# A hybrid decoder trunk on one core: the source of 48 adding transfers, and the place of a quarter's first Strassen step

## The chip, the cores and the metric

The kernel runs on one core of a Trainium2 chip. The core has TensorE (matmuls, PE in the profile, its weight loads PEld), VectorE (DVE), ScalarE (ACT), GpSimd (POOL), the sequencer SyncE (SP), which here issues plain loads, and 16 DMA engines, which all queues share. The metric is the device time of one execution in microseconds, the median over several runs.

## What is computed

The reference is a decoder of two layers over 256 tokens of width 2048, all in fp32. The first layer mixes tokens with a convolution module beside differential attention, the second with a gated short convolution. Each layer then attends to 256 memory tokens and applies an MLP whose hidden width is 8192:

```python
def sq_relu_mlp(h, w1, w2):
    return jnp.square(jax.nn.relu(h @ w1)) @ w2

for l in range(DEPTH):                     # DEPTH = 2, D_MODEL = 2048, D_FF = 8192, SEQ = 256
    hn = rms_norm(x, mix_norm_g[l])
    x = x + (even_mixer(hn, ...) if l % 2 == 0 else odd_mixer(hn, ...))
    x = x + cross_attention(rms_norm(x, xattn_norm_g[l]), mem_n, ...)
    x = x + sq_relu_mlp(rms_norm(x, mlp_norm_g[l]), mlp_w1[l], mlp_w2[l])
return rms_norm(x, final_norm_g)
```

## The kernel before

**Split numbers.** The kernel hands TensorE its factors as fp32r, a rounded fp32. To keep fp32's exactness each factor is split into `hi`, its rounded part, and `lo`, the rest, and a product is hi x hi + lo x hi + hi x lo. For a piece of weights (128 x 1024 floats, 512 KB) the helper `weights` (L152 to L170) loads `raw` from DRAM on SP's queue, ACT casts it to `whi` (L164), and DVE subtracts, `wlo = raw - whi` (L169). Of `raw` there are five buffers, of `whi` and `wlo` three each. In the order of the program a load waits until the last reader of its buffer is done.

**The adding transfer.** With `added` set, `wlo` is made without DVE: ACT writes `-raw` into it (L166), and POOL issues a DMA that adds the same piece of weights, from DRAM, onto it (L167). As both are written in fp32r, what stays is the rest. Only the second piece of 48 calls is made so, one in each Strassen step.

**A chunk.** `proj_long` makes 128 output columns from two such pieces: fifteen matmuls with `whi` (tokens' hi and lo side by side, 512 columns), sixteen with `wlo` (256 columns: hi alone), and one last with `whi`.

**The MLP** (`mlp`, L824) goes through the hidden width in four quarters, `qd`. Sixteen chunks c = 0 to 15 make a quarter's hidden activations; after each, DVE adds the two halves (L216) and multiplies (L834), ACT squares (L836). After every fourth, ACT and DVE split the result (`hid`, L840 and L841), and for Strassen's sums DVE combines it in place (L740 to L743) and splits that too (`hs`, L745 and L746). In the first three quarters eight Strassen steps follow. A step takes 256 hidden columns and multiplies half of the output (`w2[:NS]`) by seven products instead of eight: `seven_weights` loads two pieces, `raws`, combines and splits them into `shi`, `slo`, `b22` and two `tw` (L767 to L777), each single or double as the pools give, and 21 matmuls into seven PSUM banks `p` use them. Then a chunk into the bank `mmn`, with the adding transfer, makes the other half. Two layers with three such quarters give 48 steps. `shi` and `slo` share the three buffers of `whi` and `wlo`, `raws` the five of `raw`; `tw` and `b22` have one buffer each.

**What sets the order.** A scheduler puts each engine's instructions in one fixed order when the program is built: by their place in the program and by when buffers come free in its own reckoning. Where `strict` is set, PE keeps the program's order. Every engine then runs its list strictly in that order, each instruction waiting for its semaphores; SP's list holds all plain loads, so a load that waits holds up those behind it.

**Around it.** `spread` (L276) makes two diagonal tiles `diag` on ACT and multiplies each by ones on PE, to lay a row over all partitions.

Of the kernel before, what the change touches and what calls it, by code (L numbers as in the profile page):

```python
# [10 lines left out]
F32 = mybir.dt.float32  # L11
# [3 lines left out]
ALU = mybir.AluOpType  # L15
AX = mybir.AxisListType

P = 128
D = 2048
S = 256  # L20
# [7 lines left out]
NEG = -3.0e38  # L28
# [17 lines left out]
def trunk(ctx: ExitStack, tc: tile.TileContext, d):  # L46
    nc = tc.nc
    V, A, T, G = nc.vector, nc.scalar, nc.tensor, nc.gpsimd

    const = ctx.enter_context(tc.tile_pool(name="const", bufs=1))  # L50
# [4 lines left out]
    tmp = ctx.enter_context(tc.tile_pool(name="tmp", bufs=2))  # L55
    small = ctx.enter_context(tc.tile_pool(name="small", bufs=4))
    pools = {}
# [18 lines left out]
    for n in (2048, 1024, 128):  # L76
        onec[n] = const.tile([P, 1], F32, name=f"onec{n}")
        G.memset(onec[n], 1.0 / n)
    mask = const.tile([P, 2, P], F32, name="mask")
    G.memset(mask, 0.0)  # L80
    zero = small.tile([P, 1], F32, name="zero", bufs=1)
    V.memset(zero, 0.0)
    A.copy(zero, zero)
    G.affine_select(out=mask[:, 1], in_=mask[:, 1], compare_op=ALU.is_ge, fill=-NEG, base=0,
                    pattern=[[-1, P]], channel_multiplier=1)

    def col(name, c=0):
        i = VEC[name] + c
        return gvec[:, i:i + 1] if i < NG else vec[:, i - NG:i - NG + 1]
# [5 lines left out]
    def load_vec():  # L95
        nc.sync.dma_start(out=vec, in_=d["vec"][:, NG:])
        lv = vec[:, VEC["lam"] - NG:VEC["lam"] - NG + 256].rearrange("p (a b) -> p a b", a=4)
        lp = tmp.tile([P, S], F32, tag="t32", name="lp", bufs=6)[:, :128].rearrange("p (a b) -> p a b", a=2)
        V.tensor_tensor(lp, lv[:, 0:4:2], lv[:, 1:4:2], op=ALU.mult)
        ls = small.tile([P, 2], F32, name="ls", bufs=1)  # L100
        V.reduce_sum(out=ls, in_=lp, axis=AX.X)
        le = small.tile([P, 2], F32, name="le", bufs=1)
        A.activation(le, ls, AF.Exp)
        V.tensor_tensor(neglam, le[:, 1:2], le[:, 0:1], op=ALU.subtract)
        V.tensor_scalar(neglam, neglam, -LAM0, None, op0=ALU.add)
        V.tensor_scalar(subg, col("subln_g"), 1.0 - LAM0, None, op0=ALU.mult)
# [12 lines left out]
    def ordered(i, token):  # L119

        tc.stamp_issue_order_token(i.ins, token)
# [30 lines left out]
    def weights(src, added=False):  # L152

        run_later(rate[0], calls[0])
        run_stages(calls[0])
        calls[0] += 1
        raw = wraw.tile([P, 1024], F32, tag="raw", name="raw")
        hi = wspl.tile([P, 1024], F32R, tag="whi", name="whi")
        lo = wspl.tile([P, 1024], F32R, tag="wlo", name="wlo")
        n = 512 if calls[0] == 1 else 1024  # L160
        for i in range(0, 1024, n):
            o = slice(i, i + n)
            nc.sync.dma_start(out=raw[:, o], in_=src[:, o])
            A.copy(hi[:, o], raw[:, o])  # L164
            if added:
                A.activation(lo[:, o], raw[:, o], AF.Copy, scale=-1.0)  # L166
                G.dma_start(out=lo[:, o], in_=src[:, o], accum_op=ALU.add)  # L167
            else:
                ordered(V.tensor_tensor(lo[:, o], raw[:, o], f(hi[:, o]), op=ALU.subtract), "lo")  # L169
        return hi, lo  # L170
# [105 lines left out]
    def spread(rows):  # L276
        ps = ps_nm.tile([P, 512], F32, tag="nm", name="nmb")[:, :S]
        for t in range(2):
            dg = tmp.tile([P, P], F32, tag="diag", name="diag", bufs=1)
            A.activation(dg, ident, AF.Copy, scale=rows[:, t:t + 1])  # L280
            mm(ps[:, t * P:(t + 1) * P], ones, dg, start=True, stop=True)
        return ps
# [18 lines left out]
        return y  # L301

    def to_sbuf(ps, pool=None, name="rb"):
        r = pool.tile([P, S], F32, tag=name, name=name) if pool else tmp.tile([P, S], F32, tag="rb", name=name, bufs=2)
        A.copy(r, ps)
        return r

# [15 lines left out]
            V.tensor_tensor(self.acc, self.acc, sq, op=ALU.add)  # L323

    def tmp32(name="t32"):
        return tmp.tile([P, S], F32, tag="t32", name=name, bufs=6)

    def residual(k, ps, nxt, ss, gname):

# [15 lines left out]
        return softmax_from(src, nm, width, scale)  # L345

    def softmax_from(src, bias, width, scale):
        p = pools["att"].tile([P, S], F32, tag="pexp", name="pexp", bufs=3)
        sm = small.tile([P, 1], F32, tag="psum", name="psum")
        A.activation(p[:, :width], src, AF.Exp, bias=bias, scale=scale, accum_out=sm)  # L350
        inv = small.tile([P, 1], F32, tag="pinv", name="pinv")
        V.reciprocal(inv, sm)
        return p, inv
# [4 lines left out]
    def even_mixer():  # L358
        xa, ss = Act(NC, "xn"), SumSq()
        w = d["even_in"]  # L360

        def load_x(g):
            nc.sync.dma_start(out=x[:, 2 * g:2 * g + 2], in_=d["xT"][:, 2 * g:2 * g + 2])
# [22 lines left out]
        rc, r = rr["col"], rr["bc"]  # L386
        for n, pp in enumerate(pps):
            for t in range(2):
                o = slice(n * 512, (n + 1) * 512)
# [103 lines left out]
        a = half.tile([P, NA, S], F32, tag="half", name="a")  # L493
# [234 lines left out]
    NS = 8  # L728
# [54 lines left out]
                "t1": flat(t1[:, 0, 0], t1[:, 1, 0]), "t4": flat(t1[:, 0, 1], t1[:, 1, 1]),  # L783
                "t3": flat(t2[:, 0, 0], t2[:, 1, 0]), "t2": flat(t2[:, 0, 1], t2[:, 1, 1])}

    def seven_step(pp, src, sa, s, first, last):
        b = seven_weights(src)
        for i, a, w in ((1, sa.single(2 * s, 0), "b11"), (2, sa.single(2 * s + 1, 0), "b21"),
                        (5, sa.comb(1, s), "t1"), (4, sa.single(2 * s + 1, 1), "t4"), (3, sa.comb(4, s), "b22"),
                        (7, sa.comb(3, s), "t3"), (6, sa.comb(2, s), "t2")):  # L790
            mm(pp[i], a[0], b[w][0], start=first, stop=False)
            mm(pp[i], a[1], b[w][0], start=False, stop=False)
            mm(pp[i], a[0], b[w][1], start=False, stop=last)

    def seven_sum(pp, acc):

        (c11, c12), (c21, c22) = [[acc[:, i, j * 512:(j + 1) * 512] for j in range(2)] for i in range(2)]
        u = pools["mlp"].tile([P, 512], F32, tag="u", name="u", bufs=2)
        A.copy(u, pp[1])
        for out, other, op in ((c11, u, ALU.add), (c11, pp[2], ALU.add), (c12, pp[5], ALU.add),  # L800
                               (c22, pp[5], ALU.add), (c21, pp[4], ALU.subtract), (c12, pp[3], ALU.add),
                               (u, pp[6], ALU.add), (c12, u, ALU.add), (u, pp[7], ALU.add), (c21, u, ALU.add),
                               (c22, u, ALU.add)):
            V.tensor_tensor(out, out, other, op=op)
# [19 lines left out]
    def mlp(l, xa, ss, gname):  # L824
        r = rstd(ss.acc, D)
        nxt = nss = None
        w1, w2 = d[f"w1{l}"], d[f"w2{l}"]
        uu = half.tile([P, 2, 2, 4, P], F32, tag="half", name="uu")
        for qd in range(4):
            hid = Act(NC, "hid")  # L830
            sa = SevenAct(hid) if qd < 3 else None
            for c in range(NC):
                u = summed(proj_long(w1[qd * NC + c], xa))
                V.scalar_tensor_tensor(u, u, 0.0, r, op0=ALU.max, op1=ALU.mult)  # L834
                v = uu[:, c // 4 % 2]
                A.activation(v[:, c % 4 // 2, c % 2 * 2:c % 2 * 2 + 2].rearrange("p h f -> p (h f)"), u, AF.Square)  # L836
                if c % 4 == 3:
                    t = hid.t[c // 4]
                    w = v.rearrange("p a (o h) f -> p (a o) (h f)", o=2)
                    A.copy(t[:, :, 0], w)  # L840
                    V.tensor_tensor(t[:, :, 1], w, f(t[:, :, 0]), op=ALU.subtract)  # L841
                    if sa:
                        sa.combine(c // 4, v)
                if c == 1 and qd == 0:
                    acc = turned(True)
                if c == 3 and qd == 3:
                    turned(False)
            cols = slice(qd * D, (qd + 1) * D)
            if qd < 3:
                pp = {i: (ps_mm if i < 5 else ps_at).tile([P, 512], F32, tag="mm" if i < 5 else "at", name=f"p{i}")  # L850
                      for i in range(1, 8)}
                strict[0] = True
                for s in range(8):
                    o = qd * D + s * 2 * P
                    seven_step(pp, w2[:NS, :, o:o + 2 * P], sa, s, s == 0, s == 7)
                    ps = ps_nm.tile([P, 512], F32, tag="nm", name="mmn")
                    residual(NS + s, proj_long(w2[NS + s][:, cols], hid, ps, True), None, None, gname)
                seven_sum(pp, acc)
                strict[0] = False
                continue  # L860
            nxt, nss = Act(NC, "xn") if l == 0 else None, SumSq()
            for c in range(NC):
                residual(c, proj_long(w2[c][:, cols], hid), nxt, nss, gname)
        return nxt, nss
# [14 lines left out]
    r = spread(rstd_rows(ss.acc, D))  # L879
    for g in range(8):  # L880
        o = slice(2 * g, 2 * g + 2)
# [62 lines left out]
```

## Time and profile before

| | |
|---|---|
| median of three runs | 3023.36 us (3022.45 to 3029.5) |
| profiled execution | 3020.86 us, span 3019.1 us |
| PE busy | 2903.0 us (96%) |
| DVE / ACT / POOL busy | 2206.7 / 1605.4 / 45.0 us |
| mean granted TensorE clock | 0.99 |
| read from HBM | 560.3 MB |
| adding transfers | 48, 512 KB each, 8.5 us from issue to landing (median) |
| six stretches of eight Strassen steps | 618.1 us |

The span is the time between the first and last instruction in the trace. In rows of groups, a line, an engine, an operation and its tiles (written <- read) are followed by busy time, mean duration and idle time with what ended it. In rows of the timeline come the start in us, the length (over all of the row's instructions) and in brackets the idle time ahead of it with its releaser; SPq is SP's queue of issues. Rows by windows give, for each stretch, the busy time of each engine, the granted clock (PEclk), the mean busy share of the DMA engines and what they moved in GB/s. Rows of DMA queues give packets, MB and the share of the engines' time: q1 holds SP's plain loads, q0 POOL's transfers.

### The profile page before, as it was taken

To read this page: it belongs to the slowest core of one execution; us is meant where nothing else is said; L and a number is where in the kernel's file an instruction comes from. 1 tells how busy PE (TensorE), PEld (TensorE's weight loads), DVE (VectorE), ACT (ScalarE), POOL (GpSimd) and SP (SyncE) were. 2 spreads that over 40 slices of the span, in tenths; PEclk is the share of its full clock that TensorE was granted. 3 is DMA by queue.
4 is the path that set the end of the run, shared out by engine and by line. 5 is a ranking of instruction groups with operands and counts; after the bars stand their busy time and mean duration, and the time that the engine had idled before them with its cause. 6 is when DMAs were issued, how large, how long until landed. Compare 5 with 4: busy or idle time off the path is not lost.

```text
span 3019.1 us, 42397 instructions
## 1 busy us (share of the span) xinstructions
PE 2903.0 (96%) x16072; PEld 2521.6 (84%) x16072; DVE 2206.7 (73%) x3414; ACT 1605.4 (53%) x2275; POOL 45.0 (1%) x68
## 2 busy tenths in 40 slices
PE   9999999999989989999999999999999899899998
PEld 7888888888877878778888888888888787787887
DVE  7899987777776876766777765477667778777665
ACT  6665455555554545555544444455556546455453
POOL 0000000000000000000000000000000000000000
PEclk9999999999999999999999999999999999999999
DMA  7454565545576685766665656654455766757664
GB/s 242 158 198 154 181 182 189 162 151 186 182 208 187 189 222 174 206 193 188 186 194 196 202 193 193 191 189 160 153 182 181 211 191 198 202 189 212 189 187 138
DMA packets 194172, 565.17 MB, mean 187 GB/s; under 512 B 17456, under 2 KB 66736, under 8 KB 193968
## 3 DMA queue, kind: packets, MB, share of 16 engines
q1 hardware_dynamic: 187056, 537.30, 56.5%
q0 software_dynamic: 6912, 25.17, 4.3%
q8 instruction: 126, 2.06, 0.3%
q14 instruction: 78, 0.64, 0.1%
HBM read 560.30 MB, written 2.10 MB: 186 GB/s over the span
## 4 chain that ended last, share of the span: by engine, by line
PE 80%; DMA 14%; ACT 3%; DVE 2%; issue 1%; SPq 0%; ACTq 0%; DVEq 0%; POOLq 0%
PE mm L143 66%; DMA wlo<-w 13%; PE mmr L143 7%; PE mmn L143 3%; PE p L143 2%; ACT wlo L166 1%; PE pox L143 1%; PE sx L143 1%; ACT whi L164 1%; DVE wlo L169 0%; PE nmb L143 0%; ACT tw L776 0%; DVE slo L768 0%; DVE cv L511 0%; PE nmr L143 0%
## 5 line engine op out<-in xcount | busy, mean ns | idle before, releaser
L169 DVE TENSOR_TENSOR wlo<-raw,whi 128x1024 fp32r<-128x1024 f32 (+1 forms) x865 | 1057.0, 1222 | 457.5 <-PE mm L143 169.6
L164 ACT CAST whi<-raw 128x1024 fp32r<-128x1024 f32 (+1 forms) x913 | 958.4, 1050 | 667.4 <-PE mm L143 271.6
L143 PE MATMUL mm<-xn,whi 128*128 128x512 f32 x3840 | 941.8, 393 | 0.0
L143 PEld LDWEIGHTS mm<-xn,whi 128*128 128x128 f32 x3840 | 704.0, 189 | 133.5
L143 PEld LDWEIGHTS mm<-xn,wlo 128*128 128x128 f32 x3840 | 500.7, 191 | 23.7
L143 PE MATMUL mm<-xn,wlo 128*128 128x256 f32 x3840 | 508.4, 282 | 0.0
L215 ACT COPY sum<-mm 128x256 f32<-128x256 f32 x272 | 101.1, 372 | 569.0 <-PE mm L143 568.8
L143 PE MATMUL mmn<-hid,whi 128*128 128x512 f32 x768 | 192.1, 392 | 0.0
L216 DVE TENSOR_TENSOR sum<-mm,sum 128x256 f32<-128x256 f32 x272 | 115.0, 423 | 98.3 <-ACT sum L215 97.7
L143 PE MATMUL mmn<-hid,wlo 128*128 128x256 f32 x768 | 116.1, 296 | 72.2 <-DMA wlo<-w 72.1
L143 PEld LDWEIGHTS mmn<-hid,wlo 128*128 128x128 f32 x768 | 104.5, 196 | 85.7 <-DMA wlo<-w 81.9
L143 PEld LDWEIGHTS mmn<-hid,whi 128*128 128x128 f32 x768 | 145.3, 189 | 28.2
L777 DVE TENSOR_TENSOR tw<-raws,tw 128x1024 fp32r<-128x1024 f32 x96 | 114.2, 1220 | 41.3 <-ACT tw L776 41.3
L143 PE MATMUL mmr<-whi,mem 128*128 128x512 f32 x512 | 137.4, 390 | 0.0
L143 PE MATMUL p<-tw,hs 128*128 128x512 f32 x432 | 120.4, 402 | 13.1 <-ACT tw L776 6.9
L143 PE MATMUL mm<-mem,whi 128*128 128x512 f32 x512 | 126.3, 393 | 0.0
L143 PE MATMUL mm<-o,whi 128*128 128x512 f32 x512 | 124.7, 392 | 0.0
L143 PE MATMUL mm<-hid,whi 128*128 128x512 f32 x512 | 122.7, 391 | 0.0
L143 PEld LDWEIGHTS p<-tw,hs 128*128 128x128 f32 x432 | 83.9, 195 | 38.0 <-DVE tw L777 11.0
L511 DVE SCALAR_TENSOR_TENSOR cv<-a,vec,cv 128x255 f32<-128x255 f32 (+14 forms) x240 | 111.7, 465 | 3.4
L143 PEld LDWEIGHTS mmr<-whi,mem 128*128 128x128 f32 x512 | 95.8, 188 | 19.7
L143 PEld LDWEIGHTS mm<-hid,whi 128*128 128x128 f32 x512 | 94.1, 188 | 18.6 <-DVE hid L841 0.5
(208 smaller groups left out, 3304.7 us busy)
## 6 DMA issues: line engine op xcount, KB each, us to landing
raw<-w SPq DMA_DIRECT2D x416, 512.0 KB, 4.0
raws<-w SPq DMA_DIRECT2D x96, 512.0 KB, 3.9
raw<-odd_in SPq DMA_DIRECT2D x96, 512.0 KB, 4.3
raw<-even_in SPq DMA_DIRECT2D x64, 512.0 KB, 4.3
raw<-xk SPq DMA_DIRECT2D x64, 512.0 KB, 3.7
raw<-xv SPq DMA_DIRECT2D x64, 512.0 KB, 3.6
raw<-xq SPq DMA_DIRECT2D x64, 512.0 KB, 3.8
raw<-xo SPq DMA_DIRECT2D x64, 512.0 KB, 3.7
```

The lines of the kernel that those rows point to most:

```text
L143: i = T.matmul(*a, **k)
L164: A.copy(hi[:, o], raw[:, o])
L166: A.activation(lo[:, o], raw[:, o], AF.Copy, scale=-1.0)
L169: ordered(V.tensor_tensor(lo[:, o], raw[:, o], f(hi[:, o]), op=ALU.subtract), "lo")
L215: A.copy(t, ps[:, S:])
L216: V.tensor_tensor(t, ps[:, :S], t, op=ALU.add)
L511: ordered(V.scalar_tensor_tensor(cv[:, c, s:], a[:, c, :S - s], col("conv_a_w", i + j), cv[:, c, s:], op0=ALU.mult, op1=ALU.add), "lo")
L777: V.tensor_tensor(t[:, 1], b, f(t[:, 0]), op=ALU.subtract)
```

## The change

1. The adding transfer reads `raw`, the tile on chip, instead of the same piece in DRAM. Its buffer is thereby read until the transfer is through.
2. `seven_weights` is called outside `seven_step`; that of a quarter's first step is called in the loop over chunks, after chunk 12, instead of after chunk 15.
3. Buffers: `t32` 7 instead of 6, `diag` 2 instead of 1, `rb` 3 instead of 2, `pexp` 4 instead of 3, `u` 1 instead of 2. The `mask` of the causal attention is made in the pool of the attention stage instead of among the constants.

```diff
-    mask = const.tile([P, 2, P], F32, name="mask")
-    G.memset(mask, 0.0)
...
-                G.dma_start(out=lo[:, o], in_=src[:, o], accum_op=ALU.add)
+                G.dma_start(out=lo[:, o], in_=raw[:, o], accum_op=ALU.add)
...
-            dg = tmp.tile([P, P], F32, tag="diag", name="diag", bufs=1)
+            dg = tmp.tile([P, P], F32, tag="diag", name="diag")
...
-        r = pool.tile([P, S], F32, tag=name, name=name) if pool else tmp.tile([P, S], F32, tag="rb", name=name, bufs=2)
+        r = pool.tile([P, S], F32, tag=name, name=name) if pool else tmp.tile([P, S], F32, tag="rb", name=name, bufs=3)
...
-        return tmp.tile([P, S], F32, tag="t32", name=name, bufs=6)
+        return tmp.tile([P, S], F32, tag="t32", name=name, bufs=7)
...
-        p = pools["att"].tile([P, S], F32, tag="pexp", name="pexp", bufs=3)
+        p = pools["att"].tile([P, S], F32, tag="pexp", name="pexp", bufs=4)
...
+        mask = pools["att"].tile([P, 2, P], F32, name="mask", bufs=1)
+        G.memset(mask, 0.0)
...
-    def seven_step(pp, src, sa, s, first, last):
-        b = seven_weights(src)
+    def seven_step(pp, b, sa, s, first, last):
...
-        u = pools["mlp"].tile([P, 512], F32, tag="u", name="u", bufs=2)
+        u = pools["mlp"].tile([P, 512], F32, tag="u", name="u", bufs=1)
...
+                if c == 12 and sa:
+                    b = seven_weights(w2[:NS, :, qd * D:qd * D + 2 * P])
...
-                    o = qd * D + s * 2 * P
-                    seven_step(pp, w2[:NS, :, o:o + 2 * P], sa, s, s == 0, s == 7)
+                    if s:
+                        o = qd * D + s * 2 * P
+                        b = seven_weights(w2[:NS, :, o:o + 2 * P])
+                    seven_step(pp, b, sa, s, s == 0, s == 7)
```

PE's list hardly changes. Two places in the lists of the other engines do. The first is SP's list in the steps 1 and 2 of the first quarter, before; `raws` are the two pieces of a step's combined weights, `raw` the two of its chunk, and the names in brackets are semaphores: DMAHW of plain loads, DMASW of POOL's transfers.

```order
L760 DMA raws_8682<-w20 128x4x256 [waits DMAHW2_49,DVE_49]
L760 DMA raws_8683<-w20 128x4x256 [waits DMAHW5_49,DVE_49]
L163 DMA raw_8725<-w20 128x1024 [waits DMAHW4_49,DVE_49,Activation_49]
L163 DMA raw_8731<-w20 128x1024 [waits DMAHW6_49,Activation_49]
L760 DMA raws_8772<-w20 128x4x256 [waits DMAHW3_49,DVE_49]
L760 DMA raws_8773<-w20 128x4x256 [waits DMAHW1_49,DVE_49]
L163 DMA raw_8815<-w20 128x1024 [waits DMAHW7_49,DVE_49]
L163 DMA raw_8821<-w20 128x1024 [waits DMAHW2_49,Activation_49]
```

And the same rows of the changed kernel:

```order
L760 DMA raws_8682<-w20 128x4x256 [waits DMAHW2_49,DVE_49]
L760 DMA raws_8683<-w20 128x4x256 [waits DMAHW3_49,DVE_49]
L159 DMA raw_8725<-w20 128x1024 [waits DMAHW4_49,DVE_49]
L159 DMA raw_8731<-w20 128x1024 [waits DMAHW5_49,DVE_49]
L760 DMA raws_8772<-w20 128x4x256 [waits DMAHW6_49,DMASW0_49,Activation_49]
L760 DMA raws_8773<-w20 128x4x256 [waits DMAHW0_49,DVE_49]
L159 DMA raw_8815<-w20 128x1024 [waits DMAHW7_49,DVE_49]
L159 DMA raw_8821<-w20 128x1024 [waits DMAHW1_49,DVE_49]
```

The first `raws` of step 2 now waits for a DMASW, the landing of step 0's adding transfer; so does the first of each later step, two transfers back, and the three loads behind it come after it in the list. Before, a load of each step waited for ACT's copy instead.

The second place is DVE's list where the first step's weights stand, before: from the end of chunk 14's sum on.

```order
L768 TENSOR_TENSOR slo<-raws,shi 128x1024
L769 TENSOR_TENSOR raws<-raws 128x4x128
L771 TENSOR_TENSOR raws<-raws 128x4x128
L773 TENSOR_TENSOR raws<-raws 128x4x128
L169 TENSOR_TENSOR wlo<-raw,whi 128x1024
L774 TENSOR_TENSOR raws<-raws 128x4x128
L216 TENSOR_TENSOR sum<-mm,sum 128x256
L777 TENSOR_TENSOR tw<-raws,tw 128x1024
L834 SCALAR_TENSOR_TENSOR sum<-sum,rb 128x256
L777 TENSOR_TENSOR tw<-raws,tw 128x1024
```

And in the changed kernel, where `slo`, two `raws` and the split of `hid` stand ahead of this piece, right behind the sum of chunk 11:

```order
L740 TENSOR_TENSOR uu<-uu 128x2x128
L773 TENSOR_TENSOR raws<-raws 128x4x128
L741 TENSOR_TENSOR uu<-uu 128x2x128
L212 TENSOR_TENSOR sum<-mm,sum 128x256
L742 TENSOR_TENSOR uu<-uu 128x2x128
L833 SCALAR_TENSOR_TENSOR sum<-sum,rb 128x256
L743 TENSOR_TENSOR uu<-uu 128x2x128
L774 TENSOR_TENSOR raws<-raws 128x4x128
L777 TENSOR_TENSOR tw<-raws,tw 128x1024
L746 TENSOR_TENSOR hs<-uu,hs 128x8x128
L777 TENSOR_TENSOR tw<-raws,tw 128x1024
L165 TENSOR_TENSOR wlo<-raw,whi 128x1024 x3
```

The sum in it is that of chunk 12. The three `wlo` behind it are the two of chunk 13 and the first of chunk 14; before, a `wlo` stood in the middle of the piece.

More of the change, by code (lines that the diff above doesn't have):

```diff
@@ L83, in trunk @@
     A.copy(zero, zero)
-    G.affine_select(out=mask[:, 1], in_=mask[:, 1], compare_op=ALU.is_ge, fill=-NEG, base=0,
-                    pattern=[[-1, P]], channel_multiplier=1)
     def col(name, c=0):
@@ L97, in load_vec @@
         lv = vec[:, VEC["lam"] - NG:VEC["lam"] - NG + 256].rearrange("p (a b) -> p a b", a=4)
-        lp = tmp.tile([P, S], F32, tag="t32", name="lp", bufs=6)[:, :128].rearrange("p (a b) -> p a b", a=2)
+        lp = tmp.tile([P, S], F32, tag="t32", name="lp", bufs=7)[:, :128].rearrange("p (a b) -> p a b", a=2)
         V.tensor_tensor(lp, lv[:, 0:4:2], lv[:, 1:4:2], op=ALU.mult)
@@ L360, in even_mixer @@
         w = d["even_in"]
+        mask = pools["att"].tile([P, 2, P], F32, name="mask", bufs=1)
+        G.memset(mask, 0.0)
+        G.affine_select(out=mask[:, 1], in_=mask[:, 1], compare_op=ALU.is_ge, fill=-NEG, base=0,
+                        pattern=[[-1, P]], channel_multiplier=1)
         def load_x(g):
```

## The prediction

> **What bounds the kernel now.** I read the page's first part, then the waits of PE, then the step stretches by windows, one step in the timeline, and the DMA queues.
>
> ```profile
> PE 2903.0 (96%) x16072; PEld 2521.6 (84%) x16072; DVE 2206.7 (73%) x3414; ACT 1605.4 (53%) x2275; POOL 45.0 (1%) x68
> PE mmn L143 <- DMA wlo<-w: 72.1, 46, 3.7
> PE nmb L143 <- ACT diag L280: 11.7, 14, 2.9
> PE p L143 <- ACT tw L776: 6.9, 6, 1.1
> PE p L143 <- DVE tw L777: 6.2, 10, 0.7
> ```
>
> PE is busy for 96%, so PE bounds nearly all of it, and a gain can come only out of the 116 us in which it isn't (3019.1 - 2903.0). The waits (us in total, times, longest) say where these are: 72.1 us for the adding transfer, 13.1 us for the first combined weights of a quarter (6.9 + 6.2), 11.7 us for the diagonal tile.
>
> ```profile
> core 0: us, PE busy (x) PEld busy (x) DVE busy (x) ACT busy (x) POOL busy (x), PEclk, DMA share, GB/s
> 835.99:939.74 103.75, 87.65 (x426) 73.03 (x425) 76.78 (x100) 54.53 (x60) 6.97 (x8) 0.98 0.79 213
> 2336.43:2441.01 104.58, 90.46 (x426) 74.77 (x425) 76.55 (x100) 54.48 (x60) 6.82 (x8) 0.95 0.77 207
> ...
> sum 618.14, PE 532.84 PEld 442.16 DVE 459.82 ACT 326.82 POOL 41.02; mean PE 88.81 PEld 73.69 DVE 76.64 ACT 54.47 POOL 6.84
> 939.74:1029.66 89.92, 89.92 (x512) 79.26 (x512) 65.78 (x88) 50.25 (x70) 0.00 (x0) 0.99 0.56 176
> ```
>
> The first rows are two of the six stretches of eight Strassen steps, the sum is that of all six: 618.14 us, 103.0 each. The last row is sixteen chunks between two of them: PE never idles there, and a chunk takes 89.92 / 16 = 5.6 us. So the stretches hold nearly everything that can be won. One step of them:
>
> ```profile
> 861.33 0.38 SPq L760 DMA_DIRECT2D raws<-w  x1
> 862.47 3.53 SPq L163 DMA_DIRECT2D raw<-w  x2
> 863.14 0.40 PE L143 MATMUL mmn<-hid,whi 128*128 128x512 f32 x1
> 863.62 1.05 ACT L164 CAST whi<-raw 128x1024 fp32r<-128x1024 f32 x1 [2.62 <-issue]
> 864.57 1.06 ACT L166 ACTIVATE wlo<-raw 128x1024 fp32r<-128x1024 f32 x1
> 865.92 0.85 POOL L167 DMA_DIRECT2D wlo<-w  x1 [11.40 <-ACT wlo L166]
> 866.09 7.92 SPq L760 DMA_DIRECT2D raws<-w  x2
> 868.15 3.56 PE L143 MATMUL mmn<-hid,whi 128*128 128x512 f32 x15
> 871.55 1.11 PE L143 MATMUL mmn<-hid,wlo 128*128 128x256 f32 x8
> 872.38 2.36 DVE L777 TENSOR_TENSOR tw<-raws,tw 128x1024 fp32r<-128x1024 f32 x2 [1.17 <-ACT tw L776]
> 874.16 1.21 PE L143 MATMUL mmn<-hid,wlo 128*128 128x256 f32 x8 [1.49 <-DMA wlo<-w]
> 875.21 0.40 PE L143 MATMUL mmn<-hid,whi 128*128 128x512 f32 x1
> ```
>
> A step ends with its lone whi matmul: 863.54, then 875.61, so 12.07 us, of which PE waits 1.49 and works 10.6. The wait closes a ring: the last matmul frees a whi buffer, ACT casts and copies (863.62 to 865.63), POOL issues at 865.92, the transfer lands at 874.16, nine matmuls follow. 8.2 us of it is the transfer.
>
> ```profile
> q1 hardware_dynamic: 570, 0.97, 92.2%
> q0 software_dynamic: 144, 0.52, 82.8%
> q1 hardware_dynamic: 105, 0.09, 8.4%
> q0 software_dynamic: 32, 0.13, 58.8%
> 8.00:20.00 12.00, 11.92 (x47) 9.09 (x47) 10.94 (x21) 11.89 (x25) 0.00 (x0) 1.00 1.03 407
> raws<-w SPq DMA_DIRECT2D x96, 512.0 KB, 3.9
> 1241.13 0.86 POOL L167 DMA_DIRECT2D wlo<-w  x1 [12.77 <-ACT wlo L166]
> ```
>
> The first row holds all that the queues moved from 866.6 to 870.6: 0.97 MB, plain loads alone. The next two are 870.6 to 873.8: now the adding queue q0 runs, 82.8% of 3.2 us = 2.65 us of engine time. So the transfer does not take 8.2 us, it stands 4 us behind two plain loads (the second raw of the row at 862.47, issued at its end, 865.6, and the first raws at 866.09). The fourth row is 1243.8 to 1245, 2.7 us after an issue at 1241.13 that had fewer loads ahead: q0 is already at work. The start alone is thus 2.7 us or less.
>
> **The change, part by part.** The order of the queues shows that the raws load of step n+2, called A1 here, takes the buffer that step n's adding transfer now reads, and so waits for its landing. It was issued at 866.09, 0.17 us after the transfer, and ran ahead of it. After the change it cannot. Behind it in SP's queue stand A2 (the other raws), H0 and H1 (the two raw of the chunk): all wait with it.
>
> *The transfer itself.* No row shows an adding transfer from on-chip memory. Engine time now: 2.65 us against 1.29 for a plain load at the start's rate (0.524 MB / 407 GB/s), about twice, as if each engine takes in both operands. From on-chip memory it would still take in two: I take 2.65. Bounds: 1.3 (a plain load) and 5.3 (twice the present one).
>
> The Trainium skill, "DMA: Bandwidth & Descriptors", section Bandwidth, holds that HBM binds a load at about 358 GB/s and the fabric an on-chip copy at about 435. By it the transfer would take, as an estimate, 2.65 x 358/435 = 2.2 us and each step up to 0.45 us less; no run so far shows it, and the 407 GB/s of the start speak against so low a limit.
>
> *A step with PE as its bound.* 10.6 us, if the transfer lands within 6.7 us of its issue (872.66, where PE first wanted it, less 865.92). With one load less ahead: 8.2 - 1.3 to 2.2 = 6.0 to 6.9 us. That covers it, just.
>
> *The new ring.* A1 is issued at the landing; its data is through 3.5 us later (3.9 to landing less 0.4, which lie between the end of q0's window, 873.8, and PE's start); then A2, H0, H1 follow in the queue, then the next adding transfer (3.2) and 0.4. At 407 GB/s the three take 3.9 and the ring is 11.0 us; at the 241 GB/s of 866.6 to 870.6 (0.97 MB in 4 us) they take 6.5 and it is 13.6. If the transfer is served before H1, one load drops out of the ring and PE is the bound, 10.6. Back-to-back loads are nearest to the start's row, so I take 11.1. Steps 0 and 1 have no such wait: 10.7 and 11.0. Eight steps: 6 x 11.1 + 21.7 = 88.3 us.
>
> ACT waits for A1 with the shi cast, behind which its other casts stand, and DVE for those. With 11.1 us a step PE waits 0.5, so the transfer lands 9.6 us into its step and A1 2.4 us into the next one (9.6 + 3.9 - 11.1); ACT is through with its copy at 2.1 (865.63 less 863.54), so the cast is 0.3 late. DVE's last tw now ends at 874.74, 0.9 before the step does, and PE wants it some 3.3 us later still (of the 4.6 us of combined matmuls, 863.54 to 868.15, the last six use it). That hides the 0.3; without this cover it would cost 0.3 a step, 11 us in all.
>
> *The first step three chunks ahead.* It removes PE's 13.1 us, and lets the first adding transfer of a quarter go before its step begins (ACT's copy now stands ahead of the last chunk's sum). But its DVE work falls between chunks that have none to spare, in one piece:
>
> ```profile
> L777 DVE TENSOR_TENSOR tw<-raws,tw 128x1024 fp32r<-128x1024 f32 x16 | 19.0, 1220 | 6.9 <-ACT tw L776 6.9
> L768 DVE TENSOR_TENSOR slo<-raws,shi 128x1024 fp32r<-128x1024 f32 x8 | 9.8, 1226 | 6.6 <-ACT shi L767 6.5
> L774 DVE TENSOR_TENSOR raws<-raws 128x512 f32<-128x512 f32 x8 | 5.5, 691 | 0.2
> L841 DVE TENSOR_TENSOR hid<-uu,hid 128x1024 fp32r<-128x1024 f32 x1 | 1.2, 1219 | 0.0
> L740 DVE TENSOR_TENSOR uu<-uu 128x256 f32<-128x256 f32 x1 | 0.4, 420 | 0.0
> L834 DVE SCALAR_TENSOR_TENSOR sum<-sum,rb 128x256 f32<-128x256 f32 x3 | 1.3, 422 | 0.1
> ```
>
> In the new DVE order, between the sum of chunk 11 and the first wlo of chunk 13, stand slo, hid, hs and two tw (5 x 1.22), four raws (4 x 0.69), four uu and one sum with its product (6 x 0.42): 11.4 us, then that wlo, 1.22. Counted from the end of chunk 11: 0.4 for ACT's copy, 0.84 for its sum, 12.6: the wlo is there at 13.85. PE wants it in chunk 13 after fifteen whi matmuls, at 5.6 + 3.4 (868.15 to 871.55) = 9.0. So PE waits 4.9 us there, once a quarter. Bounds: 0, if DVE gets to the piece a chunk earlier (its sum of chunk 11 forbids it), and 6.
>
> *The clock.* The granted clock is 0.95 to 0.98 in the stretches: (1 - 0.97) x 103 = 3.1 us lost a quarter with 14.2 us of waits (72.1 + 13.1 over six). After it, about 7 us of waits are left, half: 1.6 us, now on PE's path.
> The Trainium skill, "TensorE: Matmul & The Clock Gate", Part 1, holds that an idle window of about 3.4 us halves the clock for the next; by it the 4.9 us wait would cost, as an estimate, 1.7 us, and six of them 10 us; the rows' 0.95 to 0.98 agree that waits are followed by a lower clock.
>
> *The small tiles.* A second diag buffer lets both diagonal tiles be made before the first is read: of 11.7 us I take 5, bounds 0 and 8. The mask moves two POOL instructions, hidden by a POOL that is busy 1%. A seventh t32, a third rb, a fourth pexp can only drop waits that PE does not show; the single u is written once a quarter, long after its last reader. Together nothing, bounds -3 and +3.
>
> **Sum.** A quarter: 88.3 + 4.9 + 1.6 = 94.8 instead of 103.0, so 8.2 x 6 = 49, and 5: 54 us. The profiled execution took 3020.9 us (span 3019.1), 2.5 under the median 3023.4. 2966.9 + 2.5 = **2969 us**.
>
> **Rivals.**
> *Full cover* (0.11). The transfer is served before H1, the ring never binds, and DVE's piece does not stop PE: 8 x 10.6 = 85 a quarter, 18 x 6 + 5 = 113, so 2910. For it: the 2.7 us start. Against it: the DVE order.
> *The ring eats the gain* (0.09): ring 12.4, 6 x 12.4 + 21.7 + 6.5 = 102.6, six quarters and the diagonal give 7 us: 3016, within 0.3%. For it: a load that starts on idle engines is slow, 3.5 us for what takes 1.29 in a row.
> *The closed ring* (0.12), slower: SP is blocked until the landing, so nothing runs ahead any more and the loads go at 241 GB/s: 13.6 a step. 6 x 13.6 + 21.7 + 6.5 = 109.8, 6.8 x 6 - 5 = 36: 3059. It decides from a ring of 12.6 on, 1.5 over mine (54 us over 36 steps). Against it: back-to-back loads ran at 407.
> *The dear source* (0.06): both reads and the write meet at one memory, 5.3 us instead of 2.65. Ring 11.1 + 2.65 = 13.75 against it: 3065. It too decides from 1.5 us more on. That the transfer is no shorter is in these two.
>
> **How the numbers follow.** The forecast has 0.62: from 2941 (10.6 a step, 0.5 of clock) to 3001 (12.0 in the six). 0.3%, some 9 us, is what a measurement here can tell. Faster: 0.62 + 0.11 = 0.73; same: 0.09; slower: 0.12 + 0.06 = 0.18. The range holds full cover and the eaten gain, 2908 to 3020, and leaves the two slower ones out.
>
> **What would show it.** Right: PE's wait for the adding transfer under 20 us in all, its landing near 6 us instead of 8.5; raws issued right after it; steps of about 11.1; PE's waits for tw gone, and in their place six of about 5 us for DVE's wlo in the chunks. Wrong: raws landing so late that PE waits for tw in the steps (the ring), q0's engine time far over 2.65 us (the source), or no wait in chunk 13.

## The result, and the profile after

The changed kernel takes 2996.5 us (median of four runs, 2989.8 to 2999.5), the kernel before beside it 3022.9: a ratio of 0.9906 with an interval of 0.9883 to 0.993. It is faster by about 28 us, half of the 54 that were forecast. The profiled execution has a span of 2997.6 us, 21.5 less than before; it took 2999.5 us, 3 above its median, and that of before 2 below its own, which is most of the difference to 28. First its engine totals and PE's waits (us in total, times, longest):

```profile
PE 2902.7 (97%) x16072; PEld 2529.8 (84%) x16072; DVE 2201.0 (73%) x3414; ACT 1605.3 (54%) x2275; POOL 44.7 (1%) x68
PE mmn L139 <- DMA wlo<-raw: 48.4, 30, 3.7
PE mm L139 <- DVE wlo L165: 23.4, 6, 3.9
PE p L139 <- DVE tw L777: 3.0, 7, 0.7
PE nmb L139 <- ACT diag L276: 2.9, 1, 2.9
```

PE's wait for the adding transfer fell from 72.1 to 48.4 us only, that for the first combined weights from 13.1 to 3.2 (3.0 and 0.2 on ACT's), and that for the diagonal tile from 11.7 to 2.9. New are six waits of 3.9 us for DVE's wlo. By windows, two of the six stretches of eight steps, their sum, and the sixteen chunks between two of them:

```profile
827.30:922.37 95.07, 86.14 (x426) 72.51 (x425) 73.14 (x97) 53.57 (x58) 6.94 (x8) 0.98 0.73 207
1018.60:1116.41 97.81, 88.70 (x426) 74.80 (x425) 73.22 (x97) 53.51 (x58) 6.79 (x8) 0.95 0.71 204
...
sum 573.76, PE 522.02 PEld 439.14 DVE 439.35 ACT 321.01 POOL 40.87; mean PE 87.00 PEld 73.19 DVE 73.22 ACT 53.50 POOL 6.81
922.37:1018.60 96.23, 92.33 (x513) 81.03 (x512) 68.85 (x91) 51.58 (x72) 0.00 (x0) 0.96 0.59 190
```

The stretches give 44.4 us (618.1 to 573.8), but the chunks take some back: 96.23 us where the same sixteen took 89.92, PE idle for 3.9 of it, where it never idled, and busy for 92.33, at a clock of 0.96 instead of 0.99. The rest lies in the opening and the middle of the program, before and after:

```profile
0.00:835.99 835.99, 819.36 (x4664) 713.76 (x4665) 672.66 (x1286) 477.18 (x794) 4.02 (x20) 1.00 0.56 180
1325.88:2336.43 1010.55, 1010.51 (x5769) 889.37 (x5769) 690.56 (x1012) 505.81 (x711) 0.00 (x0) 1.00 0.58 185
```
```profile
0.00:827.30 827.30, 817.29 (x4664) 714.97 (x4665) 671.89 (x1289) 476.84 (x796) 3.86 (x20) 1.00 0.57 183
1307.22:2325.18 1017.96, 1014.01 (x5769) 892.35 (x5768) 694.04 (x1015) 506.55 (x713) 0.00 (x0) 1.00 0.58 185
```

| place | before | after | difference |
|---|---|---|---|
| opening, with the first sixteen chunks | 835.99 | 827.30 | -8.7 |
| six stretches of eight steps | 618.14 | 573.76 | -44.4 |
| four stretches of chunks between them | 358.14 | 382.91 | +24.8 |
| middle, with sixteen chunks of layer 2 | 1010.55 | 1017.96 | +7.4 |
| tail | 196.28 | 195.67 | -0.6 |

**Chunk 13** is where a quarter pays. The timeline of the first (DVE's piece runs from the first row to the end of the second), and the clock by windows around the wait:

```profile
800.89 1.23 DVE L768 TENSOR_TENSOR slo<-raws,shi 128x1024 fp32r<-128x1024 f32 x1
...
809.98 1.22 DVE L777 TENSOR_TENSOR tw<-raws,tw 128x1024 fp32r<-128x1024 f32 x1
811.12 2.35 DVE L165 TENSOR_TENSOR wlo<-raw,whi 128x1024 fp32r<-128x1024 f32 x2
812.39 3.21 PE L139 MATMUL mm<-xn,wlo 128*128 128x256 f32 x16 [3.90 <-DVE wlo L165]
```
```profile
809.20:813.15 3.95, 0.76 (x6) 0.77 (x7) 3.95 (x4) 1.03 (x2) 0.00 (x0) 1.00 0.57 175
813.15:816.56 3.41, 3.41 (x15) 3.22 (x15) 1.63 (x3) 0.90 (x3) 0.00 (x0) 0.50 0.75 245
```

The piece is 10.3 us long (800.89 to 811.20), and the chunk's wlo stands behind it. PE waits 3.9 us, and then works for 3.41 us at a granted clock of 0.50: 1.7 us more that no row of waits names. The Trainium skill, "TensorE: Matmul & The Clock Gate", Part 1, holds that an idle window of about 3.4 us halves the clock for the next; the second row agrees, with 3.41 us at 0.50, though PE was at work for 0.76 of the 3.95 us ahead of it. Four of the six waits of 3.9 us are followed by one such stretch of 3.41 us, two by 6.83. In the four chunk stretches PE's busy time rose by 9.2 us (358.14, all of it busy before, to 367.30), 2.3 a stretch.

**The second step** is where the stretches fell short. ACT, POOL, SP and PE there:

```profile
837.40 0.40 PE L139 MATMUL mmn<-hid,whi 128*128 128x512 f32 x1
838.02 1.04 ACT L745 CAST hs<-uu 128x1024 fp32r<-128x1024 f32 x1
838.97 1.05 ACT L160 CAST whi<-raw 128x1024 fp32r<-128x1024 f32 x1
839.91 1.05 ACT L767 CAST shi<-raws 128x1024 fp32r<-128x1024 f32 x1
840.86 1.06 ACT L162 ACTIVATE wlo<-raw 128x1024 fp32r<-128x1024 f32 x1
842.23 0.86 POOL L163 DMA_DIRECT2D wlo<-raw  x1 [12.59 <-ACT wlo L162]
850.09 1.60 PE L139 MATMUL mmn<-hid,wlo 128*128 128x256 f32 x8 [2.49 <-DMA wlo<-raw]
850.11 0.94 SPq L760 DMA_DIRECT2D raws<-w  x2
```
```profile
850.70:854.11 3.41, 3.41 (x13) 2.83 (x12) 1.89 (x3) 1.99 (x2) 0.84 (x1) 0.50 0.81 262
```

The first step ends at 837.80, and the transfer is issued 4.4 us later (865.92 less 863.54, 2.4, in the step shown of before): ACT makes `hs` of the last four chunks, then whi, then the next step's shi, and only then the copy. The same order stands in all six second steps, which take 14.4 us on average. The last row of the timeline shows the new wait as forecast: the first raws of the next step but one goes out when PE gets its wlo, not 0.17 us behind the transfer's issue. The row by windows shows what PE's wait of 2.49 us, well under 3.4, brings with it: 3.41 us at half clock again. So it is behind all six second steps, whose waits are 1.9 to 3.7 us long, and it falls mostly into the third step, which has no wait of its own and still takes 11.6 us.

**The queue** in a step, where the transfer was issued at 865.81 (866 to 869, then 869 to 872.5), and the median from issue to landing:

```profile
q1 hardware_dynamic: 302, 1.01, 97.5%
q0 software_dynamic: 7, 0.03, 4.8%
q0 software_dynamic: 137, 0.50, 71.5%
```
```profile
wlo<-raw POOLq DMA_DIRECT2D x48, 512.0 KB, 7.4
```

The transfer still takes 2.65 us of engine time (0.048 x 3 + 0.715 x 3.5), from on-chip memory as from DRAM, and still begins only when the plain loads ahead of it are through, now some 3 us after its issue instead of 4.7.

### The profile page after: what moved, and what is told of

Same layout as the page of the kernel before. It is cut to its first block, busy times and chain, and to the rows that moved or that the text cites. A ratio compares the mean times of both kernels' runs of the same rounds, so it can differ in the third digit from the quotient of the medians.

```text
span 2997.6 us, 42425 instructions
## 1 busy us (share of the span) xinstructions
PE 2902.7 (97%) x16072; PEld 2529.8 (84%) x16072; DVE 2201.0 (73%) x3414; ACT 1605.3 (54%) x2275; POOL 44.7 (1%) x68
## 5 line engine op out<-in xcount | busy, mean ns | idle before, releaser
L139 PEld LDWEIGHTS mm<-xn,wlo 128*128 128x128 f32 x3840 | 507.5, 194 | 49.3 <-DVE wlo L165 25.9
L139 PE MATMUL mm<-xn,wlo 128*128 128x256 f32 x3840 | 516.8, 285 | 23.4 <-DVE wlo L165 23.4
L139 PE MATMUL mmn<-hid,wlo 128*128 128x256 f32 x768 | 111.7, 293 | 48.5 <-DMA wlo<-raw 48.4
L139 PEld LDWEIGHTS mm<-o,whi 128*128 128x128 f32 x512 | 93.7, 188 | 18.6 <-DVE o L254 0.9
```

Source lines behind the costliest of these rows:

```text
L139: i = T.matmul(*a, **k)
```

## Experiments

The ratios are against runs of the kernel before on the same chip, whose medians lay between 3022.9 and 3028.0 us. "Step 2" and so on are means over the six stretches, taken from PE's rows.

### The parts apart

```diff
- G.dma_start(out=lo[:, o], in_=src[:, o], accum_op=ALU.add)
+ G.dma_start(out=lo[:, o], in_=raw[:, o], accum_op=ALU.add)
```

> Before with one edit: the adding transfer reads the raw buffer. The held load (my theory): the first raws of step n+2 waits for the landing and is no longer ahead of the transfer, so steps 1 to 7 get some 0.9 us shorter each (12.5 to 11.6), 42 of them 35 to 40 us in all; the first steps keep their 14.8 us. Time 2980 to 2990, PE's wait for the adding transfer falls from 72 to about 40 us, its landing from 8.5 to 7.4 us. Rival, the early request carries the gain: 3010 or more here, wait for the transfer above 60 us.

Measured: 2990.7 us, just above the expected range, ratio 0.9888 (0.9868 to 0.9907): **this one edit is level with the whole change** (0.9906). Stretches 587.3 us, steps 2 to 7 at 11.9, PE's wait for the transfer 47.5 us, landing after 7.9 us. One step (its second raws and both raw go out before the transfer now):

```profile
861.27 1.55 SPq L760 DMA_DIRECT2D raws<-w  x2
863.58 1.81 SPq L163 DMA_DIRECT2D raw<-w  x2
865.24 0.84 POOL L167 DMA_DIRECT2D wlo<-raw  x1 [10.73 <-ACT wlo L166]
873.73 0.38 SPq L760 DMA_DIRECT2D raws<-w  x1
```

The early request alone (`seven_weights` of the first step after chunk 12, nothing else):

> Before with the first step of a quarter requested at chunk 12 and nothing else. My theory from the profile after: six first steps fall from 14.8 to 10.4 us (-26), six waits of 3.9 us come up in chunk 13 (+23.4), the clock loses some 6 to 10 us more, the second steps lose 2 us each (+12) because ScalarE reaches the copy for the adding transfer late: +5 to +20, so 3028 to 3043. Rival, the request is worth its 26 us and the chunk waits are hidden without the other edits: 2995 to 3010.

Measured: 3051.5 us, ratio 1.0089 (1.0072 to 1.0107): **it costs 27 us**, more than the 5 to 20 expected.

```profile
PE mmn L143 <- DMA wlo<-w: 75.3, 36, 3.5
PE mm L143 <- DVE wlo L169: 23.4, 6, 3.9
```

First steps fall from 14.8 to 10.3 us and second ones rise from 12.3 to 15.5, so the stretches win only 5 us (612.9). Against that stand 23.4 us of waits in chunk 13. Of the span's rise of 28.7 us some 10 are left. The half clock behind those waits accounts for them: eight stretches of 3.41 us (two of the six waits are followed by two), 1.7 us each, are up to 13.7 us.

The tile edits alone, and then without the second diagonal tile:

> Before with the buffer counts and the mask's place alone (seven t32, two diag, three rb, four pexp, one u). From the profile after PE's wait for the diagonal tile falls from 11.7 to 2.9 us: 3012 to 3017. Rival, these tiles are worth nothing outside the waits named: 3020 to 3026.

> The small tiles alone as in e4_small, but with one diagonal tile as before. The second diagonal tile is the whole gain of 15 us (my theory): no change against the kernel before, ratio 0.998 to 1.002, PE's wait for the diagonal tile back at 11.7 us. Rival, the rows, the temporaries or the exponentials carry part of it: 0.995 to 0.997.

Measured: 3009.4 us (seven runs, from 3001.6 to 3014.0), a little below the expected range, ratio 0.9944 (0.9924 to 0.9964), and without the second diagonal tile 3020.5, ratio 0.9985 (0.9972 to 0.9997). By the ratios the second `diag` brings 12 of 17 us, the other tiles 5 (1 to 8). The start of the first stretch says the same: 836.0 us before, 832.6 without the second tile, 821.8 with it. Eight chunks of the opening, before and with all the tiles, and PE's wait without the second `diag`:

```profile
274.79:322.31 47.52, 44.07 (x254) 38.01 (x254) 45.81 (x89) 26.97 (x49) 0.00 (x0) 1.00 0.50 165
```
```profile
267.73:309.87 42.14, 42.14 (x255) 37.40 (x254) 41.84 (x85) 26.20 (x49) 0.00 (x0) 1.00 0.55 177
```
```profile
PE nmb L139 <- ACT diag L276: 11.7, 14, 2.9
```

Without the second tile that wait is what it was. The eight chunks gain 5.4 us, 3.5 of it idle time (47.52 less 44.07) and 1.9 busy time, and the whole opening 14.2 (835.99 to 821.78): more than the 11.7 us that the row of waits held out, because PE's busy time there shrank too, from 819.36 to 815.89 (ends of matmuls are modelled, so some of it may have been waiting).

By the ratios the three parts make -34, +27 and -17 us, together -24; the whole change made -28, within the intervals. The source and the tiles without the early request then had to be the better kernel:

> Before with the new source and the small tiles, the first step not requested ahead. The parts add up (my theory): 34 us from the source and 15 from the tiles, 2971 to 2981, some 20 us below the changed kernel, and no wait in chunk 13. Rival, the early request pays once the other two edits stand: 2992 or more.

Measured: 2975.2 us, ratio 0.9831 (0.9815 to 0.9848), 23 us below the changed kernel by the ratios: the parts add.

### The source, or the buffer that it holds

Here the transfer reads DRAM as before, and a GpSimd instruction that reads one element of `raw` and of the landed `wlo` keeps `raw` until the landing:

```diff
  G.dma_start(out=lo[:, o], in_=src[:, o], accum_op=ALU.add)
+ hold = small.tile([P, 1], F32, tag="hold", name="hold", bufs=1)
+ G.tensor_tensor(hold, raw[:, 0:1], f(lo[:, 0:1]), op=ALU.add)
```

> Before with the source left in DRAM, but a one-element instruction on GpSimd that reads the raw buffer and the landed wlo, so that the raw buffer comes free only at the landing, as with the new source. The held load: the order of the queues is all that counts, so this gains what the new source alone gains, within 6 us: 2980 to 2992. Rival, the source itself: an adding transfer that reads on chip is served sooner or leaves DRAM to the plain loads; then holding the buffer alone gives nothing or loses: 3015 to 3060, with PE's wait for the transfer still above 60 us.

Measured: 3008.3 us, ratio 0.9946 (0.993 to 0.9962): half of the new source's gain. Neither side had it right, so the same instruction was put behind the on-chip source:

> Before with the on-chip source and the one-element GpSimd instruction of the run e2_hold as well. What hold alone lacked against the new source is the 0.2 us by which that instruction frees the buffer later, in some 42 ring turns (my theory): the two together give the time of hold alone, 3002 to 3012. Rival, the DRAM source itself costs: they give the time of the source alone, 2987 to 2995.

Measured: 3012.7 us, ratio 0.9947 (0.9931 to 0.9962), the same as with DRAM. With nearly equal buffer times **the source makes no difference that these intervals (some 5 us each way) can tell; what gains is that the first raws waits for the landing**. The instruction's durations in the first of the two runs (shortest, middle, longest, in ns), two of its turns, and the durations in the second run say where the other half went:

```profile
L169 POOL TENSOR_TENSOR hold<-raw,wlo x48: 179/238/1188, 848.6 to 2809.5; 128x1 f32<-128x1 f32 x48
```
```profile
861.06 0.18 POOL L169 TENSOR_TENSOR hold<-raw,wlo 128x1 f32<-128x1 f32 x1 [7.22 <-DMA wlo<-w]
861.26 2.68 SPq L762 DMA_DIRECT2D raws<-w  x2
873.55 0.57 POOL L169 TENSOR_TENSOR hold<-raw,wlo 128x1 f32<-128x1 f32 x1 [7.25 <-DMA wlo<-w]
874.15 0.93 SPq L762 DMA_DIRECT2D raws<-w  x2
```
```profile
L169 POOL TENSOR_TENSOR hold<-raw,wlo x48: 180/542/1260, 848.3 to 2813.7; 128x1 f32<-128x1 f32 x48
```

From the transfer's last packet to the next raws it takes 0.38 us with the source alone, 0.95 with this instruction and DRAM, 1.10 with it and the on-chip source (medians of 36 turns each). 0.57 to 0.72 us more in 36 turns are 20 to 26 us, about what the two lack (17 to 18). It was more than the 0.2 us expected. That this delay is the whole of the missing half was worked out, not tried.

### The two places where the early request pays

First DVE's piece in chunk 13: the vector work of `seven_weights` is cut into four parts (shi and slo, differences, first tw, second tw), written after chunks 12, 13, 14 and 15, the request itself staying at 12.

```diff
- b = seven_weights(w2[:NS, :, qd * D:qd * D + 2 * P])
+ todo = []
+ b = seven_weights(w2[:NS, :, qd * D:qd * D + 2 * P], todo)
+ for _ in range({12: 1, 13: 1, 14: 1, 15: 1}.get(c, 0) if sa else 0):
+     todo.pop(0)()
```

> The changed kernel, with the first step's weights still requested at chunk 12, but their vector work written in four parts over chunks 12 to 15, so that the chunks' own wlo stand between them on VectorE. The piece is what stops chunk 13 (my theory): its 23.4 us of waits and some 10 us of half clock behind them go, 2961 to 2973. Rival, the pair of whi and wlo buffers that the first step holds from chunk 12 on is what the chunks lack: 15 to 25 us of waits in the chunks stay, 2988 to 3000.

Measured: 2959.0 us, 2 below the expected range, ratio 0.9778 (0.976 to 0.9796). The row `mm <- DVE wlo` is gone, and the sixteen chunks take what they took before the change, with PE never idle:

```profile
916.84:1005.74 88.90, 88.90 (x513) 78.57 (x512) 67.32 (x91) 51.35 (x71) 0.00 (x0) 1.00 0.61 198
```

The pair of buffers is still held from chunk 12 on, so it was the piece. Then the second step's copy:

```diff
- A.activation(lo[:, o], raw[:, o], AF.Copy, scale=-1.0)
+ ordered(A.activation(lo[:, o], raw[:, o], AF.Copy, scale=-1.0), "act")
...
- A.copy(sh, b1)
+ ordered(A.copy(sh, b1), "act")
```

> The changed kernel, with the copy for the adding transfer ordered ahead of the next step's shi cast on ScalarE. The late copy (my theory for the second steps, 14.4 us instead of 11.0): the transfer of a second step goes 1.0 us sooner, 6 to 9 us over six: 2986 to 2992. Rival, the loads ahead of it set its landing, not its issue: 2994 to 3000, second steps still above 14 us.

Measured: 2984.7 us, ratio 0.9858 (0.9843 to 0.9872). Second steps fall from 14.4 to 11.8 us:

```profile
838.88 1.04 ACT L160 CAST whi<-raw 128x1024 fp32r<-128x1024 f32 x1
839.82 1.06 ACT L162 ACTIVATE wlo<-raw 128x1024 fp32r<-128x1024 f32 x1
840.78 1.04 ACT L767 CAST shi<-raws 128x1024 fp32r<-128x1024 f32 x1
841.19 0.86 POOL L163 DMA_DIRECT2D wlo<-raw  x1 [11.63 <-ACT wlo L162]
848.42 1.22 PE L139 MATMUL mmn<-hid,wlo 128*128 128x256 f32 x8 [0.88 <-DMA wlo<-raw]
```

One instruction's place on ACT, 1.0 us, moved PE's start on that wlo by 1.6 us from the step's begin (12.3 to 10.7) and the mean of these steps by some 2.5. Most of what the run gained is clock, not waiting: PE's waits for the transfer fell by 2 us only (48.4 to 46.1, as later steps wait more), but its busy time in the six stretches fell by 10.7 (522.02 to 511.34), and no second step is followed by half clock any more. Both repairs together:

> The changed kernel with both repairs: the first step's vector work in four parts over chunks 12 to 15, and the copy for the adding transfer ahead of the next shi cast. They stand in different places (chunk 13, the second step), so they add (my theory): 0.9778 less 0.005 of the kernel before, 0.971 to 0.975, some 2935 to 2950. Rival, a sooner second transfer only lengthens the ring behind it: 0.977 to 0.980.

Measured: 2949.8 us, ratio 0.9756 (0.9741 to 0.9771), a little short of the sum (0.973).

### What binds the later steps

```diff
- weights(src[:, g * 1024:(g + 1) * 1024], added and g == 1)
+ weights(src[:, g * 1024:(g + 1) * 1024], added and g == 0)
...
- for k in range(16):
+ for k in ((*range(8, 16), *range(8)) if added else range(16)):
```

> As e9_split_copy, but the adding transfer makes the wlo of the chunk's first half, and PE takes that half's wlo last. What binds a step now is the ring of landing, four loads and transfer (my theory): its transfer leaves some 1.5 us sooner, with the load of the second half behind it, so steps of 11.7 us come near PE's 10.3 to 10.8 and PE's wait for the transfer falls from 50 to below 25 us: 2905 to 2930. Rival, the second half's load, which now waits for the landing, takes its place: steps stay at 11.5 or more, 2940 to 2960, with PE waiting for VectorE's wlo or a whi.

Measured: 2923.1 us, ratio 0.9667 (0.9651 to 0.9683). Steps 4 to 7 take 10.7 us instead of some 11.7.

```profile
PE mmn L139 <- DMA wlo<-raw: 18.3, 20, 2.2
PE p L139 <- DVE tw L782: 8.6, 8, 1.2
```
```profile
864.90 0.40 PE L139 MATMUL mmn<-hid,whi 128*128 128x512 f32 x1
865.39 1.05 ACT L162 ACTIVATE wlo<-raw 128x1024 fp32r<-128x1024 f32 x1
866.73 0.84 POOL L163 DMA_DIRECT2D wlo<-raw  x1 [10.46 <-ACT wlo L162]
```

The copy no longer stands behind the cast of the second half; the issue comes 1.4 us after a step's end (866.73 less 865.30) instead of 2.4. From issue to landing it still takes 7.7 us (7.6 in the run before), so what the steps gained is the sooner issue. The second half's load, held instead of the first raws, did not take its place as the bound. Last, the combination of the last four chunks' activations was moved to the fourth step:

> As e10_first_half, with the combination of the last four chunks' activations (the matrices that only the seventh and eighth step use) requested in the fourth step instead of after the last chunk. Its 4.1 us of VectorE and 1.0 of ScalarE in the first step make the second step's weights late (my theory): PE's wait for tw falls from 8.6 to below 2 us and second steps from 11.9 to some 11.0, 5 to 9 us in all: 2913 to 2919. Rival, that work then delays the fourth and fifth steps by as much: 2921 to 2927.

Measured: 2925.1 us, ratio 0.9654 (0.9631 to 0.9677), not to be told from the run before it. Second steps fall from 11.9 to 10.7 us and PE's wait for tw from 8.6 to 1.4, but third and fourth steps rise from 11.7 and 10.7 to 12.1 each, as the rival had it but a step sooner, and the wait for the transfer from 18.3 to 29.9: the work moved, and its price with it.

## Why the prediction was half right

| term, us | forecast | measured |
|---|---|---|
| first step | 10.7 | 10.3 |
| second step | 11.0 | 14.4 |
| steps 3 to 7, each | 11.1 | 11.6 |
| eighth step | 11.1 | 12.7 |
| a stretch, with the clock's 1.6 | 89.9 | 95.6 |
| wait in chunk 13 | 4.9 | 3.9 |
| half clock behind it | 0 | 2.3 (mean of six) |
| tiles, in all | 5 | 14 |

By these rows a quarter came out some 7 us dearer than forecast: 3.4 for the second step, 2.5 for the steps 3 to 7, 1.6 for the eighth and 2.3 for the half clock in the chunks, less the clock's 1.6, which the measured steps hold already, the 1.0 of the shorter wait and the 0.4 of the first step.

- **What bounds it: right.** The transfer stood behind plain loads, and holding the first raws back is what shortens the steps. The runs with the new source alone, with the held buffer and with both show it, with the source itself worth nothing that they can tell.
- **The engine time of the transfer: right**, 2.65 us; neither bound (1.3 and 5.3) came about. The 2.2 us estimated from figures of the Trainium skill, "DMA: Bandwidth & Descriptors", section Bandwidth, did not come about either: from on-chip memory the queue's rows give 2.65 as from DRAM.
- **The ring: right in its form, 0.5 us a step too short** in steps 3 to 7. The landing came after 7.4 us, not near 6: H0 and H1 are still ahead of the transfer (97.5% of the engines for 3 us), only the first raws is not. Part of the 0.5 is clock: a third step has no wait and is long by the half clock that the second left. That the path from a step's end over ACT's casts to the landing still binds, the run with the transfer for the first half shows: with the issue 1.0 us sooner and the same time to landing, steps 4 to 7 fell by 1.0. An eighth step takes 1.1 us more than those before it, and its transfer's last packet comes 1.0 us later after the issue (8.2 us against 7.2); why was not tried.
- **The second step: wrong.** It was given 11.0 us because "Steps 0 and 1 have no such wait". The step that failed is the sentence on ACT: it looked at a late cast in the steady steps, and not at ACT's order in the second step, where shi stands ahead of the copy. The run with the copy first moved that one row and won some 2.5 us a step.
- **The piece in chunk 13: right**, in place, cause and number of waits, 1.0 us too long: the piece holds just the rows that were added up, but most of them start some 0.08 us before the one ahead ends, so it took 10.3 us instead of 11.4. The run with the work in four parts took it away by spreading it.
- **The clock: mis-sized, and with the wrong sign.** The sum took half of what was lost before, because half of the waits were to be left, 1.5 us a quarter to the good and 9 in all. But the lost time goes by single waits, not by their sum: one of 3.9 us in chunk 13 costs one or two stretches of 3.41 us at half clock, one of 2.49 us in a second step costs one too. PE's busy time fell by 10.8 us in the six stretches and rose by 9.2 in the chunks between them and 3.5 in the middle, so nothing was won. The prediction had a price beside its sum, 1.7 us each and 10 in all; for chunk 13 the profile after shows 13.7.
- **The small tiles: 14 us instead of 5**, the second `diag` alone some 11 to 12, above its bound of 8. The bound came from the row of waits; PE's busy time in those chunks fell as well.

The forecast won 49 us in the quarters and 5 in the tiles. The span won 7 in the quarters (21.5 less 14.2 in the opening and 0.6 in the tail) and 14 in the tiles; that the time stayed under the 3001 us of the stated range owes 9 us to tiles that gave more than their bound, which is luck. In the quarters the early request, which the working priced at about nothing over both of its sides (4.1 us a first step against 4.9 in chunk 13), costs 23 to 27 us: second steps and half clock were its two missing terms.

## What to carry to other kernels

When a request is moved ahead, follow what it issues on every engine up to the point where that engine is next waited for: here a single cast in ACT's list, and one undivided vector piece, cost more than the 13 us of waits that the move was for. A wait that is short can be dearer than it looks when it is just long enough for the clock to fall: here one of 3.9 us cost at least 5.6, and even waits of 2.5 us on an otherwise busy PE were followed by 3.41 us at half clock. And when an edit's gain could come from what it reads or from what it holds back, hold the same thing back in another way: it takes one instruction to tell.

## What was not expected of the hardware

- An adding transfer cost 2.65 us of engine time for 512 KB whether its source lies in DRAM or on chip.
- The Trainium skill, "DMA: Bandwidth & Descriptors", section Queues, rings and completion order, holds that each engine takes turns between the queues with work for it, packet by packet. In the rows of before, a transfer with few loads ahead was at work 2.7 us after its issue, but the one issued at 865.92, with two loads queued ahead, moved nothing until 870.6, 4.7 us. If it was as ready after 2.7 us as the other, the engines took no turn on its queue for some 2 us, as if the loads queued ahead went first; no run here shows when a transfer is ready.
- The one-element GpSimd instruction that waits for a transfer took between 0.18 and 1.26 us.
